# A feed-forward layer whose second product is cut into pieces between the first's, with five of eight pairs in seven products

## The chip, the cores and the metric

The kernel runs on one core of a Trainium2 chip. The metric is the device time of one execution in microseconds (us); the kernel before has a median of 2145.9 us in three runs (2145.49 to 2146.08). Differences here are told in us, and also as a share of that time.

The engines are named as the profile names them: PE is TensorE (matrix products), PEld its weight loads, DVE is VectorE, ACT is ScalarE, POOL is GpSimd, SP is SyncE, which here only issues DMAs. Each engine works through its own instructions in the order in which they stand in its queue, and waits on semaphores for the others.

## What is computed

Two layers of a decoder over 256 tokens of width 2048. Each layer is a token mixer (mLSTM in the first, RG-LRU in the second) and then a SwiGLU feed-forward block with 5632 hidden columns; the change lies almost wholly in the feed-forward block. Cut to that:

```python
def swiglu(x, w_in, w_out):
    g, u = jnp.split(x @ w_in, 2, axis=-1)      # x: 256 x 2048, w_in: 2048 x 11264
    return (jax.nn.silu(g) * u) @ w_out          # w_out: 5632 x 2048

def reference(x, ...):
    h = x
    for layer in range(DEPTH):                   # 2
        hn = rms_norm(h, norm_mix[layer])
        mix = ...                                # mLSTM or RG-LRU, with its own in and out products
        h = h + mix
        h = h + swiglu(rms_norm(h, norm_ffn[layer]), ffn_w_in[layer], ffn_w_out[layer])
    return rms_norm(h, norm_final)
```

## The kernel before

All inputs are fp32 and the products are made in a 32-bit format of TensorE that keeps fewer bits (`fp32r`). So each operand is split into a high part (ACT rounds it: `whi`) and a low part (DVE subtracts: `wlo`), and each product of two blocks is three matmuls: high by high, high by low, low by high. Every weight passes through both engines once: SP loads a tile `raw`, ACT makes `whi` of it, DVE makes `wlo` from both, PE uses both. The split of a weight tile is given a high priority (`AHEAD`), so that it stands far ahead of its use in the queues; a scheduler at build time sets the order on each engine by these priorities and by its own idea of durations, and the sizes of the buffer pools limit how far ahead it can be.

**The first feed-forward product** (`hidden`, L715 and following). The 5632 hidden columns are worked through in 11 blocks of 512, `j` = 0 to 10. For one `j` the 2048 rows of `w_in` come as 8 pairs `p` of two 128-row tiles, and of each pair 512 columns of the g half and 512 of the u half (`pairs`, one tile `raw` of 128 x 2048). There are two blocks of 128 tokens, so a pair is a 2 x 2 by 2 x 2 product of blocks. A *plain* pair makes it in eight products, 24 matmuls of 512 columns. A pair listed in `SEVENS` (1, 3 and 5) makes it in seven (the table `PRODUCTS`), 21 matmuls, at the price of sums of weight blocks: three DVE additions into the tile `sum` (L252, L255, L256), and a split of both the raw blocks (`whix`, `wlox`, 128 x 1536) and the sums (`whit`, `wlot`, 128 x 2048) where a plain pair has one split of 128 x 2048. The token side of the seven products is made once per layer (`NormPairs.pair`, tiles `p0` to `p7`). Seven accumulators P1, P2, Q3, P4, Q5, Q6, P7 hold the sums in seven of the eight PSUM banks; at the end of `j` DVE and ACT join them, apply silu and the scale `rstd`, and leave the block `v` (L728 to L746).

**The second product** (`project_out`, L436). After every third `j` (the tuple `CHUNKS`: 3, 3, 3 and 2 blocks), `v` having been turned by PE (`turn_v`, tile `tv`, the eighth bank) and split (`hh`), the rows of `w_out` that belong to these blocks are multiplied: for each quarter `q` of the 2048 output columns and each of the two token blocks `b` an accumulator `po` over 12 (or 8) row tiles, 36 (or 24) matmuls, and DVE adds it onto the residual `h` (L442). That is a stretch of PE work of its own, with 1056 matmuls a layer in all.

The operands of `w_in` and `w_out` share the tile places `raw0` to `raw3`, `whi0` to `whi2`, `wlo0` to `wlo2` and one `sum0`. At the start of the kernel all 16 tiles of the normed input are turned (`n0.quarter`, tiles `tr_m`, L333) before the first product `qk`; SP brings the input `h` in four quarters.

## Time and profile before

| what | value |
|---|---|
| median of three runs | 2145.9 us |
| the profiled execution's own time | 2144.69 us |
| its span, first to last instruction | 2142.9 us |
| granted TensorE clock, mean of the span | 0.997 |
| DVE and ACT, share of the span busy | 71% and 50% |
| read from HBM | 401.84 MB, 189 GB/s over the span |

The profiled execution lies 1.2 us under the median. A busy time is the sum of the intervals in which an engine has an instruction in work; for PE the ends are modelled, and matmuls overlap in its pipeline, so the distance from the start of one to the start of the next says what one costs when PE has nothing to wait for. In a timeline row stand the start and the duration in us, engine, line, operation, tiles (out<-in, without buffer numbers) and shapes; in a row of groups the count, the busy time and the mean ns of one, then the idle time of the engine just before them and what ended it.

### The profile page before, as it was taken

What the parts mean: (1) busy time and instruction counts of PE and PEld (TensorE: products, weight loads), DVE (VectorE), ACT (ScalarE), POOL (GpSimd) and SP (SyncE); (2) the same over time, 40 slices, a digit from 0 to 9 for tenths busy, and PEclk for the clock granted to TensorE, in tenths of its full rate; (3) what the DMA queues carried; (4) which work ended last, traced back from release to release, by engine and by line L of the source; (5) the groups of instructions that cost most, each with busy time, mean ns of one, the idle gap of its engine ahead of it and who ended that gap; (6) DMA issues with size and microseconds to landing.
All of it is one profiled execution on the core that took longest, in us unless ns stands there. A gap on an engine that the chain in (4) does not pass through costs nothing. (4 is left out here: it accounts for less than half of the span.)

```text
span 2142.9 us, 26823 instructions
## 1 busy us (share of the span) xinstructions
PE 2111.8 (99%) x10658; PEld 1783.0 (83%) x10658; DVE 1523.2 (71%) x1486; ACT 1070.9 (50%) x1040; POOL 45.1 (2%) x62
## 2 busy tenths in 40 slices
PE   8999999999999999999999999999999999999998
PEld 8988888778888888888879999777888788888886
DVE  5655556688578758866866786768857875886685
ACT  5344445555344435544555758545534543553444
POOL 0011110000000000000000000000000000000002
PEclk9999999999999999999999999999999999999999
DMA  6556656556555555565546666655656465556563
GB/s 211 165 160 178 180 181 201 184 197 207 191 196 192 197 196 188 199 202 183 201 154 176 192 187 190 209 180 189 224 182 211 159 215 177 197 196 216 177 216 118
DMA packets 211078, 405.70 MB, mean 189 GB/s; under 512 B 14520, under 2 KB 14728, under 8 KB 210824
## 3 DMA queue, kind: packets, MB, share of 16 engines
q1 hardware_dynamic: 210808, 402.94, 58.1%
q8 instruction: 83, 1.36, 0.3%
q10 hardware_dynamic: 144, 1.05, 0.1%
q14 instruction: 43, 0.35, 0.0%
HBM read 401.84 MB, written 2.10 MB: 189 GB/s over the span
## 5 line engine op out<-in xcount | busy, mean ns | idle before, releaser
L216 ACT CAST whi<-raw 128x2048 fp32r<-128x2048 f32 x198 | 378.8, 1913 | 481.6 <-PE P L706 237.4
L217 DVE TENSOR_TENSOR wlo<-raw,whi 128x2048 fp32r<-128x2048 f32 x198 | 452.1, 2295 | 212.1 <-ACT whi L216 211.9
L198 DVE TENSOR_TENSOR wlo<-raw,whi 128x1024 fp32r<-128x1024 f32 (+1 forms) x225 | 273.2, 1218 | 189.3 <-ACT whi L197 189.0
L197 ACT CAST whi<-raw 128x1024 fp32r<-128x1024 f32 (+1 forms) x225 | 234.4, 1046 | 207.4 <-PE po L270 46.5
L269 PE MATMUL po<-wlo,hh 128*128 128x512 f32 x704 | 275.2, 391 | 0.0
L268 PE MATMUL po<-whi,hh 128*128 128x512 f32 x704 | 275.0, 391 | 0.0
L270 PE MATMUL po<-whi,hh 128*128 128x512 f32 x704 | 273.6, 390 | 0.0
L216 ACT CAST whit<-sum 128x2048 fp32r<-128x2048 f32 x66 | 126.3, 1913 | 131.9 <-PE P L706 80.3
L217 DVE TENSOR_TENSOR wlot<-sum,whit 128x2048 fp32r<-128x2048 f32 x66 | 151.3, 2292 | 46.8 <-ACT whit L216 46.8
L705 PE MATMUL Q<-wlo,p_f 128*128 128x512 f32 x440 | 172.0, 391 | 5.7 <-DVE wlo L217 5.7
L704 PE MATMUL P<-whi,p_f 128*128 128x512 f32 x440 | 171.9, 391 | 1.0 <-ACT whi L216 1.0
L704 PE MATMUL Q<-whi,p_f 128*128 128x512 f32 x440 | 172.6, 392 | 0.0
L706 PE MATMUL Q<-whi,p_f 128*128 128x512 f32 x440 | 171.4, 390 | 0.0
L706 PE MATMUL P<-whi,p_f 128*128 128x512 f32 x440 | 171.3, 389 | 0.0
L705 PE MATMUL P<-wlo,p_f 128*128 128x512 f32 x440 | 171.2, 389 | 0.0
L268 PEld LDWEIGHTS po<-whi,hh 128*128 128x128 f32 x704 | 132.2, 188 | 27.6 <-ACT hh L452 0.3
L269 PEld LDWEIGHTS po<-wlo,hh 128*128 128x128 f32 x704 | 132.4, 188 | 26.4
L270 PEld LDWEIGHTS po<-whi,hh 128*128 128x128 f32 x704 | 132.1, 188 | 26.8
L216 ACT CAST whix<-raw 128x1536 fp32r<-128x1536 f32 x66 | 98.1, 1486 | 78.3 <-PE P L706 52.3
L217 DVE TENSOR_TENSOR wlox<-raw,whix 128x1536 fp32r<-128x1536 f32 x66 | 115.7, 1752 | 16.8 <-ACT whix L216 16.3
L705 PEld LDWEIGHTS Q<-wlo,p_f 128*128 128x128 f32 x440 | 82.6, 188 | 24.8 <-DVE wlo L217 8.2
L704 PEld LDWEIGHTS P<-whi,p_f 128*128 128x128 f32 x440 | 82.6, 188 | 19.6 <-ACT whi L216 2.7
(261 smaller groups left out, 4250.5 us busy)
## 6 DMA issues: line engine op xcount, KB each, us to landing
raw<-in_ffn_w_in_dram SPq DMA_DIRECT2D x352, 512.0 KB, 4.8
raw<-in_ffn_w_out_dram SPq DMA_DIRECT2D x176, 512.0 KB, 4.9
raw<-in_m_w_in_dram SPq DMA_DIRECT2D x95, 512.0 KB, 3.8
raw<-in_r_w_in_dram SPq DMA_DIRECT2D x64, 512.0 KB, 3.8
raw<-in_m_w_out_dram SPq DMA_DIRECT2D x32, 512.0 KB, 3.7
raw<-in_r_w_out_dram SPq DMA_DIRECT2D x32, 512.0 KB, 3.9
gr<-in_r_gate_w_dram SPq DMA_DIRECT2D x8, 512.0 KB, 3.8
h<-in_x_dram SPq DMA_DIRECT2D x4, 512.0 KB, 7.9
```

Of the source, the lines that this page charges most:

```text
L197: nc.scalar.copy(hi[:, i:i + step, 0:ncols], r)
L198: nc.vector.tensor_tensor(lo[:, i:i + step, 0:ncols], r, hi[:, i:i + step, 0:ncols].bitcast(F32), op=ALU.subtract)
L216: nc.scalar.copy(hi, src)
L217: nc.vector.tensor_tensor(lo, src, hi.bitcast(F32), op=ALU.subtract)
L268: nc.tensor.matmul(o, lhsT=ah[:, bs], rhs=hi, start=(k == 0), stop=False)
L269: nc.tensor.matmul(o, lhsT=ah[:, bs], rhs=lo, start=False, stop=False)
L270: nc.tensor.matmul(o, lhsT=al[:, bs], rhs=hi, start=False, stop=(k == nk - 1))
L704: nc.tensor.matmul(o, lhsT=a[0], rhs=b[0], start=start, stop=False)
L705: nc.tensor.matmul(o, lhsT=a[0], rhs=b[1], start=False, stop=False)
L706: nc.tensor.matmul(o, lhsT=a[1], rhs=b[0], start=False, stop=stop)
```

## The change

Three things, all in the code below.

1. `SEVENS` is now (2, 3, 4, 5, 6): five pairs of each `j` in seven products, three plain ones (0, 1 and 7).
2. The second product is no longer a stretch of its own. For each `j` its part (512 rows of `w_out`) is cut into 8 pieces, a quarter `q` by a token block `b`, each of four row tiles, 12 matmuls. From pair 4 of `j`+1 to pair 3 of `j`+2 one piece stands in each pair's products, two or three products ahead of the pair's end. A piece works in one PSUM bank `out`: ACT copies the piece of `h` into the bank (L816), the matmuls add onto it, ACT copies the bank back to `h` (L823); only the first piece of a layer starts from nothing and is added by DVE (L821). The last block's part (`j` = 10) still goes through `project_out`, with 4 row tiles. The turned block `tv` takes a bank of those seven that is free just then. `raw` has three places instead of four, and `w_out` has places of its own (`rawo`, `whio`, `wloo`, two tiles each of 128 x 1024).
3. At the start of the kernel only the first quarter is turned before `qk`; each next quarter follows after four of the 16 row tiles.

```diff
-SEVENS = (1, 3, 5)
+SEVENS = (2, 3, 4, 5, 6)
...
+    def turned(kind, name):
+        tags = named[kind]
+        tags.append(tags.pop(0))
+        return bank(tags[-1], name)
...
-    PLACES = ("raw0", "raw1", "raw2", "raw3", "sum0", "whi2", "whi0", "wlo0", "whi1", "wlo2", "wlo1")
+    PLACES = (
+        "raw1", "raw2", "sum0", "whi1", "wlo1", "whi2", "rawo", "whio", "wloo", "wlo2", "raw0", "whi0", "wlo0",
+    )
...
-            raw = four("raw", f"{j}_{p}", F32, 4)
+            raw = four("raw", f"{j}_{p}", F32, 3)
...
-    for q in range(4):
-        n0.quarter(q)
+    n0.quarter(0)
...
-            ps_q0 = linear_feat(w, 0, NK, n0.act, "qk00")
+            ps_q0 = linear_feat(
+                w, 0, NK, n0.act, "qk00", lambda k: n0.quarter(k // 4 + 1) if k % 4 == 3 and k < NK - 1 else None
+            )
...
-    CHUNKS = ((0, 1, 2), (3, 4, 5), (6, 7, 8), (9, 10))
...
-            for js in CHUNKS:
-                hh, hl = [], []
-                for i, j in enumerate(js):
-                    v = hidden(j)
...
-                project_out(
-                    ffn_w_out[layer][js[0] * NB:(js[-1] + 1) * NB, :], 4 * len(js),
-                    lambda k: (hh[k // 4][:, k % 4, :], hl[k // 4][:, k % 4, :]), nxt, js[-1] == FF // NB - 1,
-                )
...
+                for i, job in enumerate(work):
+                    add(*job)
+                    between(j, p, i + 1 - len(work))
...
+            def load(q):
+                tiles.clear()
+                for i in range(2):
...
+                    nc.sync.dma_start(raw, wv[:, 2 * i:2 * i + 2, q * NB:(q + 1) * NB])
+                    with tc.high_priority(offset=AHEAD):
+                        split(wh, wl, raw)
+                    tiles.extend((wh[:, k, :], wl[:, k, :]) for k in range(2))
+
+            def piece(q, b):
+                if b == 0:
+                    load(q)
+                bs = slice(b * P, (b + 1) * P)
+                hs = h[:, b, q * NB:(q + 1) * NB]
+                o = pool_of("out").tile([P, NB], F32, tag="out", name=f"out{j}{q}{b}")
+                first = fresh.pop() if fresh else False
+                if not first:
+                    with tc.high_priority(offset=AHEAD):
+                        nc.scalar.copy(o, hs)
+                for k in range(4):
+                    product(o, (hi[:, k, bs], lo[:, k, bs]), tiles[k], first and k == 0, k == 3, skip_group_check=True)
+                with tc.high_priority(offset=AHEAD):
+                    if first:
+                        nc.vector.tensor_tensor(hs, o, hs, op=ALU.add)
+                    else:
+                        nc.scalar.copy(hs, o)
...
+        def between(j, p, left):
+            if left == -2 - p % 2 and work:
+                work.pop(0)()
+            if left == 0 and p < 2:
+                if turns:
+                    turns.pop(0)()
+                run_pending()
+            if left == 0 and p == 3 and late:
+                work.extend(late.pop()())
...
+        for left in range(len(work)):
+            work.pop(0)()
+            if left > 0 and turns:
+                turns.pop(0)()
+        project_out(
+            ffn_w_out[layer][(NJ - 1) * NB:, :], 4, lambda k: (hi[:, k, :], lo[:, k, :]), nxt,
+        )
```

The built programs show what the scheduler made of it. In the names, `P7_3` is the accumulator P7 of block `j` = 3, `whit3_6` the high parts of the sums of its pair 6, `out210` the piece of block 2, quarter 1, token block 0, and `whio210`, `whio211` the two halves of the weights of block 2, quarter 1; the last number is the buffer's.

PE, block 3, in pair 6 of the kernel after: after P7 and Q5 had their first matmul each, the piece stands in the midst of them.

```order
L725 MATMUL P7_3_4992<-whit3_6_5209,p6_f0_3695 128x512
L725 MATMUL Q5_3_4852<-whit3_6_5209,p6_f0_3695 128x512
L725 MATMUL out210_5240<-whio210_5229,hh2_4843 128x512
L726 MATMUL out210_5240<-wloo210_5230,hh2_4843 128x512
L727 MATMUL out210_5240<-whio210_5229,hh2_4843 128x512
L725 MATMUL out210_5240<-whio210_5229,hh2_4843 128x512
L726 MATMUL out210_5240<-wloo210_5230,hh2_4843 128x512
L727 MATMUL out210_5240<-whio210_5229,hh2_4843 128x512
L725 MATMUL out210_5240<-whio211_5235,hh2_4843 128x512
L726 MATMUL out210_5240<-wloo211_5236,hh2_4843 128x512
L726 MATMUL P7_3_4992<-wlot3_6_5210,p6_f0_3695 128x512
L727 MATMUL P7_3_4992<-whit3_6_5209,p6_f0_3695 128x512
```

Eight matmuls of the piece stand between the first matmul of P7 and Q5, which reads the high part `whit3_6`, and the next, which reads the low part `wlot3_6`. Before, pair 6 is a plain one, and no matmul of the second product stands between those of the first.

DVE, for the pairs 5 and 6 of block 3, before and after.

```order
L252 TENSOR_TENSOR sum3_5_5134<-raw3_5_5131 128x1024
L255 TENSOR_TENSOR sum3_5_5134<-sum3_5_5134,raw3_5_5131 128x512
L256 TENSOR_TENSOR sum3_5_5134<-sum3_5_5134,raw3_5_5131 128x512
L217 TENSOR_TENSOR wlo3_4_5104<-raw3_4_5100,whi3_4_5103 128x2048
L217 TENSOR_TENSOR wlox3_5_5139<-raw3_5_5131,whix3_5_5138 128x1536
L217 TENSOR_TENSOR wlot3_5_5143<-sum3_5_5134,whit3_5_5142 128x2048
L217 TENSOR_TENSOR wlo3_6_5174<-raw3_6_5170,whi3_6_5173 128x2048
```

```order
L265 TENSOR_TENSOR sum3_5_5150<-raw3_5_5147 128x1024
L230 TENSOR_TENSOR wlox3_5_5155<-raw3_5_5147,whix3_5_5154 128x1536
L268 TENSOR_TENSOR sum3_5_5150<-sum3_5_5150,raw3_5_5147 128x512
L269 TENSOR_TENSOR sum3_5_5150<-sum3_5_5150,raw3_5_5147 128x512
L230 TENSOR_TENSOR wlot3_5_5159<-sum3_5_5150,whit3_5_5158 128x2048
L230 TENSOR_TENSOR wlox3_6_5206<-raw3_6_5198,whix3_6_5205 128x1536
L265 TENSOR_TENSOR sum3_6_5201<-raw3_6_5198 128x1024
L268 TENSOR_TENSOR sum3_6_5201<-sum3_6_5201,raw3_6_5198 128x512
L230 TENSOR_TENSOR wloo210_5230<-rawo210_5228,whio210_5229 128x1024
L269 TENSOR_TENSOR sum3_6_5201<-sum3_6_5201,raw3_6_5198 128x512
L230 TENSOR_TENSOR wloo211_5236<-rawo211_5234,whio211_5235 128x1024
L230 TENSOR_TENSOR wlot3_6_5210<-sum3_6_5201,whit3_6_5209 128x2048
```

Before, seven rows serve three pairs (4, 5 and 6), and a whole plain pair's `wlo` stands between the sums of pair 5 and their `wlot`; after, twelve rows serve pairs 5, 6 and one tile pair of `w_out`, and `wlot3_5` stands directly behind the addition on which its high part `whit3_5` depends.

ACT, for the same place, before and after.

```order
L216 CAST whix3_5_5138<-raw3_5_5131 128x1536
L216 CAST whit3_5_5142<-sum3_5_5134 128x2048
L216 CAST whi3_6_5173<-raw3_6_5170 128x2048
L729 COPY sg3_4965<-P1_3_4957 128x512
L216 CAST whi3_7_5204<-raw3_7_5201 128x2048
```

```order
L229 CAST whix3_5_5154<-raw3_5_5147 128x1536
L229 CAST whit3_5_5158<-sum3_5_5150 128x2048
L823 COPY h_73<-out200_5126 128x512
L229 CAST whix3_6_5205<-raw3_6_5198 128x1536
L816 COPY out201_5174<-h_73 128x512
L229 CAST whio210_5229<-rawo210_5228 128x1024
L823 COPY h_73<-out201_5174 128x512
L229 CAST whio211_5235<-rawo211_5234 128x1024
L816 COPY out210_5240<-h_73 128x512
L229 CAST whit3_6_5209<-sum3_6_5201 128x2048
L759 COPY ds3_4844<-P1_3_4982 128x512
L229 CAST whi3_7_5267<-raw3_7_5264 128x2048
```

Between `whix3_6` and `whit3_6` now stand five rows of the second product, among them the copy of `out201` back to `h`, which waits for PE's last matmul of that piece in pair 5.

More of the change, by code (lines that the diff above doesn't have):

```diff
@@ L228, in stream4 @@
         for kg in range(0, nk, 4):
-            raw = four("raw", kg, F32, 4)
+            raw = four("raw", kg, F32, 3)
             for i in (0, 2):
@@ L946 @@
     ffn(1, n3, Final("fin", None))
[L947 removed]
+    close_ffn("x")
 _INS = [
```

158 lines of the change are left out of this document (91 added, 67 removed).

## Prediction

> **What bounds the kernel now.** I read the page's first lines, then the waits of PE, then the busy time by windows, then the start-to-start distance of matmuls in a timeline.
>
> ```profile
> span 2142.9 us, 26823 instructions
> PE 2111.8 (99%) x10658; PEld 1783.0 (83%) x10658; DVE 1523.2 (71%) x1486; ACT 1070.9 (50%) x1040; POOL 45.1 (2%) x62
> ```
>
> PE has 31.1 us without work in 2142.9. A change can gain only by taking matmuls away or by taking these few gaps, and it loses where PE begins to wait. Where PE waits now:
>
> ```profile
> PE Q L705 <- DVE wlo L217: 5.7, 6, 1.6
> PE tr_m L333 <- DMA h<-in_x_dram: 5.7, 2, 3.6
> PE P L704 <- ACT whit L216: 4.3, 4, 1.1
> ```
>
> ```profile
> 9.20:19.40 10.20, 6.28 (x28) 5.88 (x29) 7.92 (x15) 9.63 (x22) 0.00 (x0) 0.50 0.82 249
> 404.20:452.00 47.80, 44.23 (x194) 34.74 (x194) 40.09 (x36) 25.43 (x23) 1.64 (x1) 1.00 0.66 220
> 452.00:1092.00 640.00, 637.25 (x2845) 524.85 (x2844) 478.31 (x377) 300.56 (x203) 0.00 (x0) 1.00 0.58 196
> 1462.00:2105.00 643.00, 639.24 (x2855) 526.69 (x2854) 480.23 (x380) 300.59 (x203) 0.00 (x0) 1.00 0.59 198
> ```
>
> After the length, the columns are the busy time of PE, PEld, DVE, ACT and POOL, then the granted clock and the DMAs. PE waits at the very start, at the opening of a feed-forward layer (404 to 452), and hardly in the rest of the layer (2.8 us in 640, 3.8 in 643). The DMAs at 0.6 have room, and the bytes stay the same. DVE is at 40.1 of 47.8 in the opening and 478 of 640 behind it: it is the next engine.
>
> What one matmul of 512 columns costs when nothing waits is the distance of starts, here the first and the last of 24 that follow each other:
>
> ```profile
> 712.45 0.39 PE L704 MATMUL P<-whi,p_f 128*128 128x512 f32 x1
> ...
> 717.67 0.39 PE L706 MATMUL P<-whix,p_f 128*128 128x512 f32 x1
> ```
>
> 5.22 us over 23 steps: 0.227 us (the 0.39 is its time in the pipeline).
>
> **Term 1, the products.** Two more pairs of each block in seven products, three matmuls less each, 11 blocks, two layers: 132 matmuls less, 132 x 0.227 = **-30.0 us**. The second product keeps its 1056 matmuls a layer (10 x 8 x 12 + 96). This is certain as long as PE stays full; all else is what PE waits for.
>
> **Term 2, the start.**
>
> ```profile
> 6.34 1.09 PE L333 MATMUL tr_m<-ident,h 128*128 128x128 f32 x8
> 11.02 1.97 PE L333 MATMUL tr_m<-ident,h 128*128 128x128 f32 x8 [3.59 <-DMA h<-in_x_dram]
> ...
> 19.21 0.38 PE L285 MATMUL qk<-x_m,whi 128*128 128x256 f32 x1
> 19.42 0.29 PE L286 MATMUL qk<-x_m,whi 128*128 128x256 f32 x1
> ...
> 24.54 0.28 PE L286 MATMUL qk<-x_m,whi 128*128 128x256 f32 x1
> 24.65 0.28 PE L287 MATMUL qk<-x_m,wlo 128*128 128x256 f32 x1
> ```
>
> ```profile
> 11.91 3.22 DVE L343 SCALAR_TENSOR_TENSOR x_m<-tr_m,cols,x_m 128x256 fp32r<-128x256 f32 x8
> ```
>
> All 16 tiles are turned before the first product, which starts only at 18.42 (in the timeline); the third and fourth quarter of `h` are waited for. With the first quarter alone ahead, DVE has its low parts by about 13.5 (four of the eight rows from 11.91), and PE can multiply from about 12.5 until 18.4. But the clock is at 0.50 there (window above) and a matmul of 256 columns takes 0.21 us (19.21 to 19.42) where later it takes 0.11. 5.9 us hold 28 matmuls, which save 28 x 0.11 = **-3.2 us**. Bounds: 0, if the next quarters are late in turn, and -5.9, the whole time.
>
> The Trainium skill, "TensorE: Matmul & The Clock Gate", section "What's actually happening", says that an idle window of some 3.4 us halves PE's clock and a busy one restores it. The trace agrees: 3.6 us idle, then 0.50 until 19.4. By that rule PE, busy from 12.5, would get its clock back about one window earlier, an estimated 1.7 us more than the -3.2; I stay with the rows.
>
> **Term 3, the opening of a layer.** DVE rows by groups, then ACT:
>
> ```profile
> L217 DVE TENSOR_TENSOR wlo<-raw,whi 128x2048 fp32r<-128x2048 f32 x198 | 452.1, 2295 | 212.1 <-ACT whi L216 211.9
> L198 DVE TENSOR_TENSOR wlo<-raw,whi 128x1024 fp32r<-128x1024 f32 x223 | 271.9, 1223 | 182.0 <-ACT whi L197 181.7
> L217 DVE TENSOR_TENSOR wlot<-sum,whit 128x2048 fp32r<-128x2048 f32 x66 | 151.3, 2292 | 46.8 <-ACT whit L216 46.8
> L217 DVE TENSOR_TENSOR wlox<-raw,whix 128x1536 fp32r<-128x1536 f32 x66 | 115.7, 1752 | 16.8 <-ACT whix L216 16.3
> L252 DVE TENSOR_TENSOR sum<-raw 128x1024 f32<-128x1024 f32 x66 | 80.5, 1220 | 24.2 <-DMA raw<-in_ffn_w_in_dram 23.8
> L255 DVE TENSOR_TENSOR sum<-sum,raw 128x512 f32<-128x512 f32 x66 | 45.4, 687 | 1.0
> L743 DVE SCALAR_TENSOR_TENSOR v<-v,rstd_f,sg 128x512 f32<-128x512 f32 x44 | 32.1, 746 | 0.0
> ```
>
> ```profile
> L216 ACT CAST whi<-raw 128x2048 fp32r<-128x2048 f32 x198 | 378.8, 1913 | 481.6 <-PE P L706 237.4 <-PE po L270 183.2 <-issue 56.2
> L197 ACT CAST whi<-raw 128x1024 fp32r<-128x1024 f32 x223 | 233.1, 1050 | 206.5 <-PE po L270 46.5 <-PE qk L286 43.8 <-PE v L270 39.5
> L319 ACT ACTIVATE junk<-h 128x512 f32<-128x512 f32 x40 | 25.4, 635 | 39.2 <-DVE h L442 35.5 <-DMA h<-in_x_dram 3.0
> L729 ACT COPY sg<-P 128x512 f32<-128x512 f32 x22 | 12.7, 576 | 0.0
> ```
>
> ```profile
> 404.24 0.39 PE L704 MATMUL Q<-whi,p_f 128*128 128x512 f32 x1
> ...
> 461.97 0.60 PE L753 MATMUL tv<-ident,v 128*128 128x128 f32 x4
> ```
>
> ```profile
> 390.99 0.29 DVE L403 TENSOR_TENSOR c_f<-c_f 128x128 f32<-128x128 f32 x1
> ...
> 393.07 1.09 DVE L217 TENSOR_TENSOR p_f<-c_f,p_f 128x896 fp32r<-128x896 f32 x1
> ...
> 406.28 1.23 DVE L252 TENSOR_TENSOR sum<-raw 128x1024 f32<-128x1024 f32 x1
> ...
> 429.61 1.22 DVE L252 TENSOR_TENSOR sum<-raw 128x1024 f32<-128x1024 f32 x1
> 430.75 1.75 DVE L217 TENSOR_TENSOR wlox<-raw,whix 128x1536 fp32r<-128x1536 f32 x1
> ```
>
> A pair in seven products costs DVE 1.22 + 0.69 + 0.69 + 1.75 + 2.29 = 6.6 us and PE 21 x 0.227 = 4.8; a plain one 2.3 and 5.4. As block 0 has no pieces of the second product, five such pairs in a row are bound by DVE. Its first sum stands behind the last additions onto `h` in both kernels, 2.0 us after PE's first product (404.24, 406.28). Up to the last `wlot` of block 0 the new order has 5 x 6.6 = 33.2 us, two tiles of `w_out` 2.4, two plain splits 4.6 and the last two norm tiles about 3.5 (rows like those at 390.99 and 393.07): 43.7. Rows that don't depend on each other start some 0.08 before the end of the one ahead (429.61 to 430.75 is 1.14, not 1.22), 2 us in all; and the first `wlot` waits some 1.3 for ACT, whose cast stands behind a norm tile. So it ends 2.0 + 43.7 - 2.1 + 1.3 = 44.9 us after PE's start, and 20 matmuls (4.5) follow: 49.4. PE's own work is 177 x 0.227 + 0.7 for turning = 40.9: a stall of 8.5. Before, PE needed 57.7 us (404.24 to 461.97) for 231 matmuls and the turning, 53.1: a stall of 4.6. **+3.9 a layer, +7.8 in all**; bounds +2.6 (no ACT wait) and +6.0 (no overlap) a layer.
>
> **Term 4, the blocks behind it.** What goes is the 2.8 + 3.8 = 6.5 us of PE's gaps in the two windows, most of them at the first pairs after a stretch of the second product. What comes is read from the sums. Per block PE has 273 matmuls and the turning, 62.8 us; DVE 33.2 + 3 x 2.29 + 8 x 1.22 for `w_out` + 6.3 to join the seven sums + 1.4 = 57.6; ACT 5 x 3.4 + 3 x 1.91 + 8 x 1.05 + 16 copies of 0.58 to 0.64 + some 3 = 44. The copy of `h` into a bank isn't in the trace; 0.58 (from a bank, L729) and 0.64 (from SBUF, L319) bound it. All fit, but in the pairs 2 to 6 DVE only keeps pace: 6.6 + 1.2 per pair by durations against 33 x 0.227 = 7.5. The tightest place is pair 6 of the order shown: from the end of piece `out201` ACT has the copy to `h`, a cast, the copy into the bank and `whit3_6`, 0.58 + 1.05 + 0.6 + 1.91 = 4.1, then DVE's `wlot3_6`, together 6.1 to 6.4; PE has 9 + 9 + 2 + 8 matmuls until it needs that, 6.4. Hand-overs come on top: I take 0.3 us a block, 20 blocks, +6. Bounds 0 and 1.4 (both tight places of a block, pairs 5 and 6, by durations with their hand-overs), so 0 to +28. Net **-0.5**.
>
> **Term 5, the ends.** Behind the last block the pieces `out920` and `out921` stand with little between; the one bank has to be copied out and in, 1.2 and hand-overs: 1.3 a layer, **+2.6** (bounds 0 and 5 a layer).
>
> ```profile
> 2130.76 0.69 DVE L442 TENSOR_TENSOR h<-po,h 128x512 f32<-128x512 f32 x1 [6.79 <-PE po L270]
> ...
> 2134.45 0.68 DVE L442 TENSOR_TENSOR h<-po,h 128x512 f32<-128x512 f32 x1
> ```
>
> At the very end the second token block's addition (2134.45) stands behind the first's work; with four row tiles instead of eight the first ends 12 matmuls ahead of PE's end, not 15: **+0.7**.
>
> **Sum.** -30.0 - 3.2 + 7.8 - 0.5 + 2.6 + 0.7 = -22.6 against the profiled execution's 2144.7: 2122.1. The median of the runs is 1.2 above it: **2123 us**.
>
> **The rivals.**
>
> *DVE becomes the bound (slower).* Place: pairs 2 to 6 of every block. `wlot3_5` stands directly behind the addition that its high part waits for, so DVE stands for ACT's 1.91. Were it so in all five pairs, DVE's block would be 57.6 + 9.5 = 67.1, 4.3 over PE's 62.8, 20 blocks: +86 in place of the +6, 2203 us. It decides from 5.2 us of DVE idle a block; the time is over the old one from 1.4 us of PE stall a block (22.6 + 6 over 20). For it: `wlot` waits 0.7 us a time now (46.8 over 66) with far less behind it. Against: in pair 4 `wlox` stands between and covers most of it, and PE's order puts pieces where the low parts are late. 12%.
>
> *ACT's queue is the link (no change).* The casts stand behind copies that wait for PE's pieces; if both tight places cost their upper bound, 1.4 a block, the gain is gone: 2123 - 6 + 28 = 2145. 10%.
>
> *The clock closes in an opening.* If DVE's lag gathers into one gap as long as that at 7.4 to 11.0, PE falls to 0.50 for 10.2 us (the window 9.20:19.40), 5.1 us of work lost a layer: 2133. The gaps that I find are near 2 us each. 4%. This is the rule of the Trainium skill's "TensorE: Matmul & The Clock Gate" again; a layer's windows show 1.00 now.
>
> *The stalls are hidden wholly*: -30.0 - 5.9 + 5.2 - 6.5 + 0.7 = -36.5, 2109. 6%.
>
> That the change doesn't do what it says I exclude: the built order has the products and pieces as told.
>
> **The numbers.** Forecast 68%, then 12, 10, 4 and 6. The forecast's own upper end is term 4's bound, 2123 + 22 = 2145; the range reaches 2110 to 2148 and leaves out the slow rival and the edges. Faster by over 0.2% (4.3 us, about what a measurement of this kernel can tell) is forecast, clock and hidden stalls: 0.78; within it 0.10; slower 0.12.
>
> **What would show it.** In the profile after: 132 matmuls less at 0.227 us; PE's windows in the layers with gaps near 8 us in each opening and 0.3 a block; DVE near 90% in the layers; the waits of PE led by `wlo` and `wlot`; `qk` starting near 12.5. It is wrong if PE's waits on DVE or ACT pass 20 us in the windows behind the openings, or if the copies between `out` and `h` are waited for by PE.

## The result and the profile after

| kernel | median, us | runs | ratio to before, 95% interval |
|---|---|---|---|
| before, beside it | 2145.99 | 4 | |
| changed | 2167.18 | 4 | 1.0101, 1.0088 to 1.0114 |

The change makes the kernel 21 us slower, where 2123 us were forecast, 23 us faster. The profiled execution took 2166.43 us, 44.3 over the sum of the prediction (2122.1). All ratios here are of executions in the fast state; one of the four executions of e2 below was slow (3651 us, at a mean granted clock of 0.563) and is not in its ratio. These are the first lines of the page of the changed kernel:

```profile
span 2164.6 us, 27306 instructions
PE 2108.3 (97%) x10526; PEld 1758.9 (81%) x10526; DVE 1682.3 (78%) x1704; ACT 1308.3 (60%) x1480; POOL 43.0 (2%) x62
```

The 132 matmuls are gone (10658 to 10526), but PE's busy time fell by 3.5 us only, not by 30, and its idle time grew from 31.1 to 56.3. Busy time that does not fall with the work says that PE ran slower or in many short waits, which a modelled busy time swallows. The view of PE's waits (engine, line and tile, what it waited for, us in total, times, longest):

```profile
PE P L725 <- ACT whit L229: 6.4, 6, 1.6
PE P L726 <- DVE wlot L230: 5.0, 4, 1.4
PE P L726 <- DVE wlox L230: 4.9, 6, 1.4
PE out L725 <- ACT out L816: 4.5, 6, 1.1
PE qk L298 <- ACT x_m L354: 4.4, 1, 4.4
PE P L725 <- ACT whi L229: 4.0, 2, 2.0
PE rec L298 <- ACT whi L208: 3.9, 1, 3.9
```

Where they lie is read from the busy time by windows (length, then PE, PEld, DVE, ACT, POOL, the granted clock, the DMAs and GB/s). The first four rows are the first layer from its first product to the first turning of `v`, from there to the turning of the next block, over eight blocks more, and the opening of the second layer; the others are the three stretches between the kernel's start and its end in which the granted clock was 0.50:

```profile
401.70:464.70 63.00, 52.18 (x210) 39.54 (x209) 51.20 (x50) 33.23 (x30) 1.63 (x1) 0.95 0.43 143
464.70:523.30 58.60, 56.11 (x246) 44.76 (x245) 54.16 (x48) 33.47 (x31) 0.00 (x0) 1.00 0.59 197
523.30:1034.70 511.40, 508.81 (x2249) 413.33 (x2248) 440.53 (x377) 333.58 (x337) 0.00 (x0) 1.00 0.60 198
...
1429.90:1492.60 62.70, 52.31 (x210) 39.45 (x209) 51.24 (x50) 33.23 (x30) 1.60 (x1) 0.95 0.44 143
...
447.70:454.50 6.80, 5.76 (x14) 4.50 (x15) 4.41 (x3) 0.99 (x1) 0.00 (x0) 0.50 0.95 343
1133.80:1140.60 6.80, 5.59 (x24) 5.21 (x25) 5.18 (x7) 3.54 (x4) 0.69 (x1) 0.50 0.44 134
1475.10:1481.90 6.80, 6.12 (x14) 4.33 (x15) 5.22 (x3) 1.85 (x2) 0.00 (x0) 0.50 0.94 317
```

Their edges are the starts of these matmuls in the timeline (start, duration, engine, line, tiles); the time from one turning to the next is the length of a block, whatever PE's modelled ends say:

```profile
401.70 0.39 PE L725 MATMUL Q<-whi,p_f 128*128 128x512 f32 x1
...
464.75 0.60 PE L780 MATMUL tv<-ident,ds 128*128 128x128 f32 x4
...
523.32 0.60 PE L780 MATMUL tv<-ident,ds 128*128 128x128 f32 x4
...
1034.72 0.60 PE L780 MATMUL tv<-ident,ds 128*128 128x128 f32 x4
```

The opening holds 201 matmuls up to the turning (177 of block 0, 24 of block 1): 45.6 us at 0.227, so 17 of its 63.0 are lost. About 3 of them go to the half clock: PE was busy for 5.76 us of those 6.80, and at full clock half of that would have done. Block 1 holds 237 (only five pieces stand between these two turnings): 53.8 and 0.8 for the turning, so 4.0 are lost. The eight blocks behind take 63.9 each for 62.8 of work.

Why the opening is so long is seen in DVE's timeline. Each row is a DVE operation, the bracket the wait ahead of it:

```profile
403.74 1.23 DVE L265 TENSOR_TENSOR sum<-raw 128x1024 f32<-128x1024 f32 x1
...
407.27 0.69 DVE L269 TENSOR_TENSOR sum<-sum,raw 128x512 f32<-128x512 f32 x1
410.08 2.29 DVE L230 TENSOR_TENSOR wlot<-sum,whit 128x2048 fp32r<-128x2048 f32 x1 [2.12 <-ACT whit L229]
...
413.43 1.22 DVE L265 TENSOR_TENSOR sum<-raw 128x1024 f32<-128x1024 f32 x1
...
419.91 2.29 DVE L230 TENSOR_TENSOR wlot<-sum,whit 128x2048 fp32r<-128x2048 f32 x1 [1.52 <-ACT whit L229]
...
423.12 1.22 DVE L265 TENSOR_TENSOR sum<-raw 128x1024 f32<-128x1024 f32 x1
...
437.17 0.69 DVE L269 TENSOR_TENSOR sum<-sum,raw 128x512 f32<-128x512 f32 x1
440.50 2.29 DVE L230 TENSOR_TENSOR wlot<-sum,whit 128x2048 fp32r<-128x2048 f32 x1 [2.64 <-ACT whit L229]
```

From one pair's first sum to the next it is 9.7 us, not the 6.6 that the durations of a pair add up to; PE needs 4.8 for the pair. Of the difference, 2.1 and 1.5 us are the waits ahead of `wlot`; most of the rest are a tile of `w_out` in the first pair and norm tiles in the second. Three of the five `wlot` wait for ACT, 6.3 us together. Each of these stands behind the last addition into its own `sum` with at most 0.6 us of other work between, so that DVE has nothing to do while ACT casts `whit`; ahead of the other two stand other splits, and they don't wait.

The eight blocks behind are not alike. In each layer six take 63.3 to 63.5 us and two, every third one, 64.9 to 65.7. In these two, and in no other, DVE's order has the first sum of the next block among the rows that join the accumulators (`ds`), and that sum waits for its weights from DMA:

```profile
701.31 0.68 DVE L760 TENSOR_TENSOR ds<-Q,ds 128x512 f32<-128x512 f32 x1
703.80 1.23 DVE L265 TENSOR_TENSOR sum<-raw 128x1024 f32<-128x1024 f32 x1 [1.81 <-DMA raw<-in_ffn_w_in_dram]
704.94 0.68 DVE L761 TENSOR_TENSOR ds<-P,ds 128x512 f32<-128x512 f32 x1
```

PE then waits for the joined accumulators. These are its only waits on record in the eight blocks, 2.6 us in the first layer and 2.1 in the second. Why those weights are late no run shows; that `raw` has three places instead of four is one possible reason, and no run varies it.

### The profile page after: what moved, and what is told of

The parts are those of the page before. It is cut to its first block, busy times and chain, and to the rows that moved or that the text cites. A ratio compares the mean times of both kernels' runs of the same rounds, so it can differ in the third digit from the quotient of the medians.

```text
span 2164.6 us, 27306 instructions
## 1 busy us (share of the span) xinstructions
PE 2108.3 (97%) x10526; PEld 1758.9 (81%) x10526; DVE 1682.3 (78%) x1704; ACT 1308.3 (60%) x1480; POOL 43.0 (2%) x62
## 4 chain that ended last, share of the span: by engine, by line
PE 86%; DVE 4%; ACT 4%; issue 3%; DMA 2%; SPq 0%; POOL 0%; ACTq 0%; DVEq 0%; POOLq 0%
PE P L726 7%; PE P L725 6%; PE P L727 6%; PE out L725 6%; PE out L726 6%; PE out L727 6%; PE Q L725 5%; PE Q L726 5%; PE Q L727 5%; PE po L281 3%; PE po L282 3%; PE po L283 3%; DMA raw<-in_ffn_w_in_dram 2%; PE qk L298 1%; PE qk L299 1%
## 5 line engine op out<-in xcount | busy, mean ns | idle before, releaser
L229 ACT CAST whio<-rawo 128x1024 fp32r<-128x1024 f32 x160 | 168.5, 1054 | 144.2 <-PE out L727 141.9
L725 PE MATMUL out<-whio,hh 128*128 128x512 f32 x640 | 250.3, 391 | 4.5 <-ACT out L816 4.5
L726 PE MATMUL out<-wloo,hh 128*128 128x512 f32 x640 | 249.9, 390 | 1.1 <-DVE wloo L230 1.1
L727 PE MATMUL out<-whio,hh 128*128 128x512 f32 x640 | 249.4, 390 | 0.0
L230 DVE TENSOR_TENSOR wloo<-rawo,whio 128x1024 fp32r<-128x1024 f32 x160 | 194.1, 1220 | 9.4 <-ACT whio L229 9.1
L823 ACT COPY h<-out 128x512 f32<-128x512 f32 x158 | 92.7, 586 | 171.9 <-PE out L727 171.9
L230 DVE TENSOR_TENSOR wlo<-raw,whi 128x2048 fp32r<-128x2048 f32 x74 | 168.2, 2296 | 13.2 <-ACT whi L229 13.1
L229 ACT CAST whi<-raw 128x2048 fp32r<-128x2048 f32 x74 | 139.9, 1915 | 48.1 <-PE P L727 26.8
L725 PEld LDWEIGHTS out<-whio,hh 128*128 128x128 f32 x640 | 120.1, 188 | 32.8 <-ACT out L816 7.5
L265 DVE TENSOR_TENSOR sum<-raw 128x1024 f32<-128x1024 f32 x110 | 134.2, 1220 | 8.8 <-DMA raw<-in_ffn_w_in_dram 7.8
L727 PEld LDWEIGHTS out<-whio,hh 128*128 128x128 f32 x640 | 120.1, 188 | 25.5
L725 PE MATMUL P<-whi,p_f 128*128 128x512 f32 x264 | 104.4, 395 | 6.9 <-ACT whi L229 4.0
L725 PE MATMUL Q<-whi,p_f 128*128 128x512 f32 x264 | 105.8, 401 | 1.9 <-DVE ds L764 1.9
L727 PE MATMUL P<-whi,p_f 128*128 128x512 f32 x264 | 104.0, 394 | 0.0
```

What stands on the lines that cost most here:

```text
L229: nc.scalar.copy(hi, src)
L230: nc.vector.tensor_tensor(lo, src, hi.bitcast(F32), op=ALU.subtract)
L265: nc.vector.tensor_tensor(t[:, 0:2, :], raw[:, 1:3, :], raw[:, 3:4, :].broadcast_to([P, 2, NB]), op=ALU.add)
L725: nc.tensor.matmul(o, lhsT=a[0], rhs=b[0], start=start, stop=False, **kw)
L726: nc.tensor.matmul(o, lhsT=a[0], rhs=b[1], start=False, stop=False, **kw)
L727: nc.tensor.matmul(o, lhsT=a[1], rhs=b[0], start=False, stop=stop, **kw)
```

## The experiments

Each kernel ran beside the kernel before on the same chip, whose median was 2145.1 to 2145.4 in all of them. "Block 1" and "the blocks" are told by the distance of the turnings, as above; the loss in an opening is the time from the first product to the first turning less its matmuls.

### e1: the pieces alone

```diff
-SEVENS = (2, 3, 4, 5, 6)
+SEVENS = (2, 4, 6)
```

> The changed kernel with three pairs of each block in seven products (2, 4, 6) in place of five: the second product's pieces, the copies of h through the bank and the new start stay, only DVE's and ACT's load of the sums goes back to that of before. Theory A (the loss is DVE's: five pairs in seven products with no pieces between them, in block 0 and the first half of block 1, and the clock that the long gaps close): 132 matmuls come back, +30.0 us, the openings' stalls fall from 17 us a layer to some 5 (-24), block 1's 6.7 us a layer go (-13), so about 2155 to 2160, and no granted clock of 0.50 in the feed-forward layers. Theory B (the pieces themselves cost it: copies through the one bank, ACT's queue): the stalls stay, 2190 to 2197.

Measured: 2139.44 us, ratio 0.9971 (0.9960 to 0.9982). The pieces, the copies of `h` through one bank and the new start are, with three pairs at other places than before, together a gain of 6 us. Theory A holds and was too careful: the openings take 50.2 us with 207 matmuls (47.0), each of the eight blocks 64.3, PE's busy time is the whole of that stretch, and the clock stays at 1.00 in both layers. Theory B falls. What the edit takes away is the load of DVE and of ACT together, so it doesn't say which of them binds.

```profile
509.70:1024.40 514.70, 514.70 (x2297) 424.88 (x2296) 374.47 (x312) 312.38 (x321) 0.00 (x0) 1.00 0.58 196
```

### e2: five pairs alone, in the kernel before

```diff
-SEVENS = (1, 3, 5)
+SEVENS = (2, 3, 4, 5, 6)
```

> The kernel before with five pairs in seven products (2 to 6) and nothing else changed: the second product stays a stretch of its own behind three blocks. Theory A: three blocks need DVE for 3 x 46.4 = 139 us against 3 x 40.2 = 121 us of PE, so some 12 to 18 us of stall for each group of three, four groups a layer, against -30 for the products: 2190 to 2230, slower than the changed kernel; the pieces are what makes five pairs bearable. Theory B (the pieces are what costs): faster than before, 2116 to 2135.

Measured: 2362.46 us, ratio 1.1005 (1.0987 to 1.1024). Theory A's sign, far beyond its size. PE's waits in that kernel:

```profile
PE P L704 <- ACT whix L216: 59.7, 40, 1.6
PE P L705 <- DVE wlox L217: 40.7, 59, 1.4
PE P L704 <- ACT whi L216: 30.3, 22, 1.5
PE P L704 <- ACT whit L216: 18.2, 18, 1.1
```

They are 149 us. A single wait is 1.6 us at most, yet the clock fell to 0.50 eighteen times between start and end and was 0.980 on the mean. The waits are led by `whix`, not by `whit`, and with the half clock they explain most of the 217 us but not all. In the order of the kernel before, five pairs in seven products are not fed; with the pieces between them nearly all of this loss is gone.

### e3: the pieces two pairs earlier

```diff
-            if left == 0 and p == 3 and late:
+            if left == 0 and p == 1 and late:
...
+        while turns:
+            turns.pop(0)()
```

> The changed kernel with the pieces of a block's second product from pair 2 of the next block to pair 1 of the one after, two pairs earlier; the number of instructions is the same. Theory A: block 1 has pieces in its pairs 2 and 3 too, so its stall of 6.7 us falls to 1 to 3, and at the layer's end two pieces stand loose behind the last block in place of four, 2 to 3 us less: -6 to -8 a layer, 2151 to 2156. Theory B: the pieces cost the same wherever they stand: 2165 to 2168.

Measured: 2170.35 us, ratio 1.0114 (1.0099 to 1.0129). Both theories missed, A by far: block 1 takes 65.3 us in the first layer with two pieces (5.4 us) more, so it loses 5.2 instead of 4.0, and the clock closes for 13.7 us in the opening ahead of it instead of 6.8. More work for PE did not help; the weights of the pieces have to be split by the same two engines, which is the likely reason, not a shown one.

### e4: block 0 plain

```diff
+SEVENS0 = (6,)
+BOTH = (2, 3, 4, 5)
...
-            if p not in SEVENS:
+            if p not in (SEVENS if j else SEVENS0):
...
+            if p in BOTH:
+                et = pool_of("e").tile([P, 2, 3, P], F32R, tag=f"e{p}", name=f"e{p}_{self.name}")
...
+                split(et[:, 0, 0, :], et[:, 1, 0, :], c[:, 0, :])
+                split(et[:, 0, 1:3, :], et[:, 1, 1:3, :], c[:, 4:6, :])
```

The places of `w_out`'s weights are opened behind block 0, where the tiles `e` are free again.

> The changed kernel with pairs 2 to 5 of block 0 plain in both layers (their token tiles are made in both forms, three more 128x128 tiles a pair), pair 6 and all later blocks as in the changed kernel. 4 x 3 x 0.227 = 2.7 us more of products a layer. Theory A: the opening's stall of 17 us a layer, with 3.4 of it at half clock, falls to about 3, so -11 a layer, 2144 to 2148, and the clock stays at 1.00 in both openings. If the stall comes from the norm's tail and not from the sums, -3 at most a layer and the products on top: 2164 to 2172.

Measured: 2137.48 us, ratio 0.9961 (0.9946 to 0.9975): 30 us less than the changed kernel, for 5.4 us more of products, and 6.5 below the range of theory A. The windows of its first layer, cut as above:

```profile
401.30:450.50 49.20, 49.20 (x222) 40.72 (x221) 35.59 (x33) 29.12 (x27) 0.73 (x1) 1.00 0.51 173
450.50:509.40 58.90, 56.22 (x246) 44.61 (x245) 55.69 (x50) 33.49 (x31) 0.00 (x0) 1.00 0.62 213
509.40:1020.80 511.40, 508.85 (x2250) 413.31 (x2249) 440.68 (x377) 333.77 (x337) 0.00 (x0) 1.00 0.59 198
```

The opening has 213 matmuls (48.4 and the turning) in 49.20 us: nothing is lost and the clock stays open. It is shorter by 13.8 and 13.5 us in the two layers, 27 of the 30. Block 1 and the eight blocks are as in the changed kernel, so they don't lose because the opening was late. The edit also takes two tiles of `w_out` (2.4 us of DVE) out of the opening; e1 and e12, which keep them there and lose 2.4 and 11.5 us with three and four pairs, show that the pairs decide.

### e5: another order of ACT's casts

```diff
                 with tc.high_priority(offset=AHEAD):
-                    both = halves(f"{j}_{p}", raw)
+                    if "whit" in last:
+                        with tc.issue_after(last["whit"].ins):
+                            both = halves(f"{j}_{p}", raw)
+                    else:
+                        both = halves(f"{j}_{p}", raw)
...
```

(`last["whit"]` is the cast of the last `whit` before, that of pair 6.)

> The kernel of e4 (block 0 plain) with one rule more for the build's order on ACT: the casts of the plain pairs 7, 0 and 1 stand behind whit of pair 6. In e4 every third block has whi of pairs 7 and 0 ahead of it, and these blocks take 65.0 to 65.7 us where the others take 63.3 to 63.5 (distance of the turnings). If the order is the cause, six blocks win 2.0 us each: -12, 2125.5. If DVE's load of a whole block sets it (some 57 of 64 us) and the order only shows where the lack surfaces, the 2 us come out in other blocks: 2134 to 2138.

Measured: 2146.87 us, ratio 1.0007 (0.9998 to 1.0016), 9 us more than e4. Both expectations fell. The four long blocks (not six, as was expected) came down from some 65.4 to 64.7, a third of what their order was to bring, and block 1 went from 58.9 to 64.2 and 63.1: with `whi` of pair 7 held back behind `whit` of pair 6, PE stood 2.5 us for that `whit` and the clock closed. In the eight blocks no sum waits for DMA any more and none stands among the joins. So the order is part of the cause; turning it round moves the wait.

### e6: four pairs in seven products

```diff
-SEVENS = (2, 3, 4, 5, 6)
+SEVENS = (2, 4, 5, 6)
```

on e4, with pair 3 plain everywhere and `BOTH = (2, 4, 5)`.

> The kernel of e4 with four pairs in seven products (2, 4, 5, 6) in blocks 1 to 10, block 0 as in e4. Three matmuls more in each of 20 blocks, 20 x 0.68 = +13.6 us of PE work. If DVE and ACT are too tight with five, a block falls from 64.1 on average to 63.5 or 63.6 (work 62.8 + 0.7, no waits, as the blocks of e1 with three show: 64.3 against 64.2) and block 1's 4 us of stall to some 2: 2125 to 2129. If PE's products set the time, 2148 to 2151.

Measured: 2128.29 us, ratio 0.9923 (0.9907 to 0.9940), as expected. The windows of block 1 and of the eight blocks behind it:

```profile
451.90:507.70 55.80, 55.80 (x249) 45.63 (x248) 50.03 (x44) 32.37 (x30) 0.00 (x0) 1.00 0.60 206
507.70:1017.10 509.40, 509.40 (x2274) 420.36 (x2273) 408.70 (x344) 324.26 (x329) 0.00 (x0) 1.00 0.58 199
```

With 24 matmuls more than in e4, the eight blocks take 2.0 us less, and PE is busy in all of them; block 1 loses nothing. The fifth pair costs more than its three matmuls are worth.

### e7: a second bank for the loose pieces

```diff
-                o = pool_of("out").tile([P, NB], F32, tag="out", name=f"out{j}{q}{b}")
+                o = misc(f"out{j}{q}{b}") if loose else pool_of("out").tile([P, NB], F32, tag="out", name=f"out{j}{q}{b}")
...
+            loose[:] = [1] * (left % 2 == 0)
```

> The kernel of e4 with every second of the four loose pieces at the end of a layer in a bank of the first product's that is free then, so that the copies out of and into the bank stand beside the other's matmuls. The trace of e4 shows gaps of 1.1 and 0.6 us there, and 0.8 in the second layer ahead of them. If the one bank is the cause: -3, 2134 to 2135. If something else holds the pieces (the turnings, the weights): 2137.

Measured: 2130.10 us, ratio 0.9932 (0.9917 to 0.9947), 7.4 less than e4, more than expected. From the turning of the last block to the layer's end it is 4.9 and 4.4 us less, the stretch before it grows by 1.4 a layer, so the ends win 3.0 to 3.5 each. The rest lies in the second mixer (4.2 less) and in block 1 (1.6 more a layer), which the edit doesn't touch: in e4 the clock closes at the start of the second mixer and in no block 1, here it closes in block 1 of both layers and not at the mixer.

### e8: the pieces earlier, with block 0 plain

The edit of e3 on e4.

> The kernel of e4 with the pieces two pairs earlier, as in e3 (where it won nothing, but behind an opening that was late already). Block 1 takes 58.9 us in e4 where its products, its five pieces and the turning are 54.6. If pairs 2 and 3 lack work of PE's to cover DVE's sums, two more pieces (5.4 us) cost only 2 to 3 there: -5 in all, 2131 to 2133, with block 1 at 61 to 62. If DVE is full from the opening on (it is 97% busy from 445 to 505 us), the pieces bring their own casts and block 1 takes 64.3 or more: 2137 to 2140.

Measured: 2143.07 us, ratio 0.9991 (0.9981 to 1.0000), above both ranges; the profiled execution is the slowest of the ten, 2148.82. The pieces brought their own load: block 1 takes 66.3 and 68.0 us there. But the expectation's reason, DVE alone, is not shown: DVE is busy for 57.27 of those 66.3, and the waits of PE name ACT as well.

```profile
PE P L741 <- DVE ds L782: 5.3, 4, 1.5
PE P L741 <- ACT whi L231: 4.9, 2, 2.5
```

### e9 and e10: put together, and the order at the first layer's end

e9 is e6 with e7's bank. e10 adds one rule for ACT:

```diff
                 self.quarter(q)
-                self.stats(q)
+                if q == 3 and self.name == "m1":
+                    with tc.issue_after(made["w"].ins):
+                        self.stats(q)
...
```

(`made["w"]` is the second cast of the second mixer's weights.)

> e6 (four pairs in seven products, block 0 plain) with e7's second bank for the loose pieces at a layer's end. If the two gains are apart, 2128.3 - 7.4 = 2121, with the end of the first layer (last turning of block 9 to the first product of the second mixer) shorter by 4 us. If e7's gain came from another order of the whole layer and not from the bank, 2125 to 2130.

> e9 with one rule more for ACT: the last sums of squares of h at the end of the first layer stand behind the first two casts of the second mixer's weights. In the changed kernel, e3 and e6 they stand ahead of them and wait there for the last addition onto h, and PE stands 4.3 us from the last turning of h to the first product; where the build put a cast ahead (before, e1, e4, e7) it is 0.23. If that order is the cause: the gap falls to about 0.3 and the granted clock of 0.50 behind it goes, -4 to -7 against e9. If PE waits there for h itself: no change.

Measured: e9 2126.34 us, ratio 0.9916 (0.9899 to 0.9932): the end of the first layer is 4.6 us shorter than in e6 and that of the second 3.2, but the block ahead is 2.4 longer in both, so the ends win 2.2 and 0.8, and by the medians 2.0 of e7's 7.4 us are left. The bank is thus worth some 1 to 3.5 us a layer, less with four pairs than with five. e10 2121.65 us, ratio 0.9891 (0.9877 to 0.9906): the order was the cause of the late start. In the changed kernel ACT's rows there read:

```profile
1132.08 0.63 ACT L334 ACTIVATE junk<-h 128x512 f32<-128x512 f32 x1 [1.66 <-DVE h L458]
...
1132.84 0.63 ACT L334 ACTIVATE junk<-h 128x512 f32<-128x512 f32 x1
...
1133.47 2.92 ACT L208 CAST whi<-raw 128x1024 fp32r<-128x1024 f32 x3
```

The cast of the next mixer's weights, whose data had landed by 1103, stands behind two sums of squares that wait for the last addition onto `h`; PE waits 3.9 us (the row `rec` of its waits), and the clock closes. In e10 the gap from the last matmul of `po` to the first of `rec` is 1.2 us where e9 has 4.6, and the half clock lasts 3.4 instead of 6.8. e10 is the fastest kernel of this study, 24 us under the kernel before; its page:

```profile
PE 2101.1 (99%) x10610; PEld 1778.6 (84%) x10610; DVE 1577.4 (74%) x1612; ACT 1276.2 (60%) x1464; POOL 41.2 (2%) x62
```

### e11: the opening's sums on POOL

```diff
-                nc.vector.tensor_tensor(
+                adds = nc.vector if j else nc.gpsimd
+                adds.tensor_tensor(
```

> The changed kernel with the sums of weight blocks of block 0 alone (three additions a pair, 2.6 us of DVE) made on POOL in both layers; products and order of the source as in the changed kernel. PE's way from the first product to the first turning is 63.0 us in the changed kernel, with 46.2 of work. If DVE's own work binds in the opening, 13 us less of it bring this to 50 to 55 (2141 to 2152), unless POOL takes over twice as long as DVE for a sum. If the waits are for ACT's order and for one sum tile at a time, the longer way over POOL makes it worse: 65 or more, 2170 and up.

Measured: 2197.68 us in one run. The opening grew to 77.1 and 75.8 us. Taking the sums off DVE did not help, as the second theory had it; but the two engines also slow each other (last section), so how much is the longer chain and how much that is not told apart.

### e12: four pairs in every block, block 0 too

The edit of e6's first line, on the changed kernel.

> The changed kernel with four pairs in seven products (2, 4, 5, 6) in every block and nothing else changed: block 0 keeps them too, and the last sums of squares stay ahead of the second mixer's first casts. Blocks 1 to 10 as in e6 (63.7 us in place of 64.1, block 1 at 55.8 in place of 58.6): some -6 a layer. In block 0 the pairs in seven products take 9.7 us each of DVE and ACT in the changed kernel (start of one sum to the next: 403.74, 413.43, 423.12) against 4.8 of PE; one less takes 9.7 - 5.4 - 2.3 = 2 to 5 us of the 16.8 of stall away: 57 to 60 from the first product to the first turning, -3 to -6 a layer. Together 2143 to 2149, against 2128.3 with block 0 plain (e6): half of the loss is block 0's, half the other blocks'. If one pair less cures block 0 as it cures the others: 2133.

Measured: 2148.98 us, ratio 1.0017 (1.0007 to 1.0026), at the edge of what was expected. The opening takes 58.5 and 57.7 us, 4.5 and 5.0 less, and the clock still closes in it; the other blocks are as in e6. One pair fewer cures the blocks that have pieces and does not cure block 0, which still loses 11 us.

### e13 and e14: ACT's copies taken away, DVE loaded instead

```diff
-                first = fresh.pop() if fresh else False
+                first = True
```

on e4 (e13) and on e10 (e14): every piece starts from nothing and DVE adds it onto `h`.

> The kernel of e4 (block 0 plain, five pairs in seven products behind it) with every piece of the second product added onto h by DVE, as the first piece of a layer is: ACT's two copies a piece go (16 x 0.59 = 9.4 us a block of ACT's some 42), DVE gets 8 x 0.69 = 5.5 us a block on its 55. If ACT's queue (casts behind copies that wait for PE) is what five pairs strain, every block takes 63.2 and block 1 some 56: 2137.5 - 12 - 5 = 2120. If DVE's load is the limit, 60 of 63 us and over all blocks at 65 to 67: 2165 to 2195.

> The same on e10 (four pairs, block 0 plain, second bank, the order at the first layer's end), where DVE has 51 us a block and no waits: with 5.5 us more it is at 57 of 63.7. If DVE's load is the limit with five pairs at some 55 to 57 us, the blocks wait here too: 64.5 or more, 2135 to 2150. If ACT's queue was the limit, no change in the blocks: 2119 to 2123.

Measured: e13 2140.22 us, ratio 0.9973 (0.9964 to 0.9983); e14 2122.17 us, 0.9895 (0.9878 to 0.9911), no different from e10. e13 fits neither of its ranges. With five pairs and no copies the blocks take 63.9 each, all alike: the pattern of every third block is gone, no sum stands among the joins and none waits for DMA; but the mean has not moved, since now DVE is nearly full. One block of e13:

```profile
573.00:637.00 64.00, 63.84 (x283) 51.88 (x282) 59.28 (x56) 33.68 (x26) 0.00 (x0) 1.00 0.57 197
```

DVE is busy 93% of it. Relief for ACT at the price of DVE gives nothing with five pairs. With four, DVE takes the same additions, and PE is busy in all of the eight blocks of e14:

```profile
506.60:1015.80 509.20, 509.20 (x2274) 420.44 (x2273) 446.79 (x410) 257.36 (x200) 0.00 (x0) 1.00 0.59 199
```

DVE's busy time there is 55.8 us a block, more than in e4, where PE waits (440.68, 55.1 a block). So neither DVE's load nor ACT's alone tells whether PE waits; what is left is the order and the waits between a sum, its cast and its split, which no run varies alone. A second tile for the sums, which would loosen that chain, was not run.

## Why the prediction was wrong

The forecast and what came, each against the profiled executions; a layer's two figures are first and second layer:

| part | forecast, us | measured, us | missed, us |
|---|---|---|---|
| start: first product of the first layer against 404.24 | -3.2 | -2.5 | 0.7 |
| opening: first product to first turning (49.4 + 24 x 0.227) | 54.8 | 63.0, 62.7 | 16.1 |
| block 1: 237 matmuls, turning, 0.3 | 54.9 | 58.6, 58.6 | 7.4 |
| blocks 2 to 9: 8 x 63.1 | 504.8 | 511.4, 510.8 | 12.6 |
| last matmul of `po` to the first of `rec` | as before, 1.1 | 4.3 | 3.2 |
| from there to the second layer's first product | as before, 290.7 | 295.4 | 4.7 |
| the rest | | | -0.4 |

That is 44.3 us. The shares are told by starts of matmuls; the half clock, about 3 us each time, is in the two openings and in the last row but one.

**Term 1 was right.** 132 matmuls less, and where nothing waits they are worth what was said: e1's eight blocks and e6's differ by 24 matmuls and by 514.7 - 509.4 = 5.3 us, 0.22 each.

**Term 2 was right within its bounds**, -2.5 for -3.2, partly by luck: in the other kernels with the new start the first layer begins 0.9 to 3.0 us earlier than before, and the low clock there lasts 3.4 or 6.8 us. The rule of the Trainium skill that was weighed there ("TensorE: Matmul & The Clock Gate", section "What's actually happening") would have given 1.7 more. The low clock did end early, at 14.2 us instead of 19.4. But PE waits 4.4 us ahead of its first product for the high parts of the first quarter (`x_m`), which ACT makes only at 10.4, behind casts of the first weights.

**Term 3 failed at the step "the first `wlot` waits some 1.3 for ACT".** The five pairs were added up as DVE's durations with one wait of ACT's. In fact three of five `wlot` waited, 6.3 us. Sum, `whit`, `wlot` and the next sum are a chain over two engines that work in order: where nothing stands between a sum and its `wlot` on DVE, DVE stands for ACT's cast of 1.9 us. Two of the three waits are little else; the third has 0.7 more, as a copy of the accumulator P1 stood ahead on ACT. This is the mechanism that the prediction had named as its first rival, and it let block 0 have one wait of it. The last `wlot` ended at 452.1, not at 446.6: 5.5 us of the miss of 8.2. Nearly all of the other 2.7 is the half clock: 14 matmuls stood between PE's last wait (448.74) and the first that needs this `wlot` (454.72), and took 6.0 us where 3.2 would do. Pair 7's weights, for which ACT waited 2.7 us at 443.2, may have a share in that stretch that no run prices apart. Term 3 has a slip besides: the old opening holds 228 matmuls, not 231, so the old stall was 5.3, not 4.6. e4, e1 and e12 show that the pairs in seven products there are the cause: with one of them nothing is lost, with three 2.4 us, with four 11.5, with five 17.

**The rival of the closing clock was real and was given too little a chance**, 4%, with one condition wrong. It came in both openings and at the second mixer's start, about 3 us each time instead of 5.1 in each layer; that the three together are near the 10 us of the rival is luck. The prediction asked for one gap as long as 3.6 us and saw gaps of 2; in the first opening the clock closed on waits of 1.1 to 2.0 us that stood close together. The start of the kernel before could have told: the prediction read it as 3.6 us idle and then 0.50, but in its own rows the gap lies from 7.4 to 11.0 and the clock is at 0.50 from 9.2 on. The 3.4 us ahead of 9.2 had 1.7 us of PE work in them.

**Term 4 failed at "0.3 us a block x 20".** Block 1 was counted with the others, though its pairs 2 and 3 have no piece between them: 4.0 us lost, not 0.3. In the eight others 1.1 were lost on the mean, within the bound of 1.4 that was kept for the range but not in the value chosen. Some 0.2 of it was mis-sized work: e6's 63.7 less 276 x 0.227 leaves 1.0 for the turning, not 0.8. In six of the eight blocks the 0.3 was then nearly right (0.3 to 0.5). The two long ones lose 1.9 to 2.7 each: there the joins stand behind a sum that waits for DMA. The built order that the text shows ahead of the prediction is block 3's alone. The rival on DVE named a wait that came: in the eight blocks of the first layer `wlot` waits 54.3 us for `whit`, 6.8 a block, more than the 5.2 from which it was to decide. But DVE's rows take 55.1 us a block, not 57.6, and the two together still fit in 62.8. e6 shows the point from which it all fits: with four pairs nothing is lost.

**Term 5 had the loose pieces within its bounds** (1.3 a layer, where a second bank wins 2.2 and 0.8 in e9, 3.5 and 3.0 in e7) **and missed the first layer's end.** ACT's casts for the second mixer stand behind the last sums of squares in the built order; the prediction looked at the ends of both layers only for the pieces and the last addition. That cost 3.2 us of waiting and 4.7 behind it, most of it half clock; e10 wins 4.7 of them back. In e1, e4, e5, e7, e8 and e13 the build put a cast ahead without being told to, and the gap is 0.2.

Of the signs that the prediction named, DVE near 90% came (81% to 92% in the layers), and `wlot` is near the top of PE's waits, behind `whit`, which was not named, while the `wlo` of plain pairs is not among them. The openings have 10.8 and 10.4 us without PE work, not 8, and lose 17. One sign of being wrong came too: PE waits for a copy of `h` into `out`, six times, 4.5 us in all (the row `out` of its waits), 2.9 of them at the layers' ends and 1.6 in block 1.

## What to carry to other kernels

Two engines that both have room by their sums can still be late together, when each waits for the other within one step of work: add up such a chain with its waits, and compare it with the distance at which its results are needed. Look for the blocks that lack the cover that the steady ones have (the first, the second, the last), and price them apart; of the kernels run here, the best keep the plain form in the first block and use seven products in four pairs of eight, not five. And where a built order is at hand, read it on each engine at every seam of the program, not only where the change is meant to act.

## What the runs showed of the hardware

**The clock closes on a half-idle stretch; no long gap is needed.** Wherever the granted clock falls to 0.50 between the first and the last instruction of a kernel here, it is for 3.4 us or a multiple of it; only the last such stretch is cut off by the end. These windows of 3.4 us of the changed kernel stand just ahead of such a stretch (second and third row) or of none (first and fourth):

```profile
440.90:444.30 3.40, 2.27 (x10) 1.57 (x9) 3.33 (x3) 1.13 (x1) 0.00 (x0) 1.00 0.41 157
444.30:447.70 3.40, 1.38 (x5) 0.48 (x3) 3.37 (x4) 3.40 (x3) 0.00 (x0) 1.00 0.24 43
1130.40:1133.80 3.40, 0.25 (x2) 0.00 (x0) 2.36 (x7) 1.71 (x6) 0.00 (x0) 1.00 0.00 0
1468.30:1471.70 3.40, 1.82 (x7) 1.23 (x8) 2.95 (x2) 0.63 (x2) 0.00 (x0) 1.00 0.67 259
```

In e4 a stretch with 1.81 us of PE in it closed the clock:

```profile
1120.40:1123.80 3.40, 1.81 (x13) 1.21 (x11) 2.23 (x5) 1.41 (x3) 0.21 (x1) 1.00 0.65 221
```

So about half of 3.4 us decides, as far as modelled ends can tell: over all kernels here the 3.4 us ahead of a fall held 0 to 1.9 us of PE work, and some that held 1.5 to 1.9 closed nothing. The Trainium skill ("TensorE: Matmul & The Clock Gate", section "What's actually happening") has the half rate begin after at least one idle window of some 3.4 us. The length of the window agrees; that it must be idle does not.

**POOL and DVE slow each other down when both work on fp32 tiles.** In e11, a single run, POOL's groups of sums (both layers), and the groups of DVE in the first opening:

```profile
L266 POOL TENSOR_TENSOR sum<-raw 128x1024 f32<-128x1024 f32 x10 | 29.9, 2986 | 41.0 <-DVE wlot L230 41.0
L269 POOL TENSOR_TENSOR sum<-sum,raw 128x512 f32<-128x512 f32 x10 | 20.3, 2027 | 0.8
...
L230 DVE TENSOR_TENSOR wlox<-raw,whix 128x1536 fp32r<-128x1536 f32 x5 | 14.1, 2810 | 1.3 <-ACT whix L229 1.3
L230 DVE TENSOR_TENSOR wlot<-sum,whit 128x2048 fp32r<-128x2048 f32 x4 | 9.2, 2292 | 12.5 <-ACT whit L229 12.5
```

`wlox` takes 2.81 us on the mean beside POOL's sums, where the changed kernel has 1.75; `wlot`, which runs when POOL has nothing to do, keeps its 2.29. POOL is slowed too: an addition of 128x512 took it 1.3 us with DVE idle and up to 3.3 beside DVE's work. A sum of 128x1024 took it 2.4 us with DVE idle and 2.99 on the mean, where DVE needs 1.22.
